# A hybrid decoder layer: 336 series of zero products ahead of the first stage

## The chip, the cores and the metric

The kernel runs on one core of one Trainium2 chip. The metric is the device time of one execution in microseconds. The core has a matrix engine (PE, with its own sequencer that also loads weights, shown as PEld), a vector engine (DVE), a scalar engine (ACT), a general engine (POOL) and a queue engine (SP) that issues transfers. The time of the kernel before is the median of two runs, 1093.47 us (1092.93 to 1094.01).

## The reference

One inference step of one layer, for a prompt group (1 x 512 tokens) and a sample group (8 x 8 tokens) that share weights of width 1024. In float32:

```python
x -> x + post(Wout[concat(Mamba2-SSD heads, mLSTM heads)](pre(x)))   # one combined input projection
  -> x + post(CrossAttn(pre(x), memory K/V))
  -> x + post(SwiGLU(pre(x)))                                        # sandwich RMSNorm everywhere

u = _rms(x) * g_pre_mix
proj = u @ w_in
z, xbc, dt_raw, q, k, v, ig, fg, og = jnp.split(proj, split_at, axis=-1)
xbc, conv_new = causal_conv(xbc, conv_buf, conv_w, conv_b)
```

What matters here is the first step, the normalised input times `w_in`. Both groups are computed together, as 512 + 64 = 576 token columns. Besides the two outputs the step returns the new states and the memory keys and values.

## The kernel before

Activations lie feature-major: 128 partitions by 8 blocks of features by 576 token columns. Each weight matrix is taken in units of 128 x 1024, that is eight 128 x 128 tiles side by side. To reach float32 accuracy with the fast float32r products, a weight `w` is split into `whi` (rounded to float32r, by ACT) and `wlo` (the rest, by DVE or POOL), and the activation `u` likewise into `uh` and `ul`. One block of a matrix product is then three products into one PSUM bank: `whi` with `uh`, `whi` with `ul`, `wlo` with `uh` (lines 202, 203 and 205, in `gemm`; lines 339 to 341 in the first stage). A bank holds 512 float32 columns, so the 576 columns are taken as `HALVES` of 256 and 320, in the feed-forward part as two of 288, and for the values 512 at a time (line 815). No float32r product has a moving operand under 256 columns; the transposes and some small products of the recurrences are plain float32 or bfloat16.

The order at the start is this. DVE writes zeros into a small bfloat16 tile `wz` (line 300), and PE runs 21 products with it into a PSUM tile `ps_warm` that nobody reads (line 303). Meanwhile SP and ACT issue the loads of the parameters, of the input `xraw` by blocks, and of the first two units of `w_in` in quarters (`raws`, lines 304 to 314). ACT and DVE turn each block of the input into `uh` and `ul` (lines 322 and 323) and each quarter of a weight unit into `whi` and `wlo` (line 328, by way of lines 191 and 192). The loop of lines 333 to 341 then runs the first two units' products block by block into four PSUM tiles `ps_in`, and the next unit follows through `gemm`. The rest of the input projection, the convolution, the gates, the recurrences, the output projection, cross attention and the feed-forward part come behind.

SBUF is handed out in numbered slots by the helper `SL`: a tile of a slot waits for the readers of the tile before it in that slot. Slot 1 is first used in the input projection, by `qk` (the queries and keys of the mLSTM heads), when the fifth tile of the convolution is due. PSUM tiles come from rings: `MP` takes one of three banks in turn, `GP` one of three others. The order of instructions on each engine is chosen when the program is built, by a scheduler that simulates a timeline; blocks under `tc.manual_schedule` keep the written order on the engines that they name, and `tc.issue_after` sets an order between two instructions.

```python
    wz = sp.tile([P, 256], BF16, name="wz")
    V.memset(wz, 0.0)
    psw = MP("ps_warm")
    for _ in range(NWARM):
        mm(psw[:, 0:256], wz[:, 0:128], wz, start=True, stop=True, skip_group_check=True)
    S.dma_start(par, I["par"])
```

Of the kernel before, what the change touches and what calls it, by code (L numbers as in the profile page):

```python
# [11 lines left out]
F32 = mybir.dt.float32  # L12
F32R = mybir.dt.float32r
# [6 lines left out]
P = 128  # L20
# [95 lines left out]
def build(nc, tc, ctx, I, O):  # L116
    V, A, G, S, TE = nc.vector, nc.scalar, nc.gpsimd, nc.sync, nc.tensor
    mm = TE.matmul
# [12 lines left out]
    def SL(slot, name, dt=F32, shape=(P, KT, T)):  # L131

        return big.tile(list(shape), dt, name=name, tag="s%d" % slot, bufs=1)
# [5 lines left out]
    def MP(name="m"):  # L139
        return pa.tile([P, 512], F32, name=name, tag="a")  # L140
# [54 lines left out]
    def gemm(ps, units, xh, xl, t0, n, k0=0, k1=None, order=None, late=0):  # L195


        tiles = [(hi[:, j * P:(j + 1) * P], lo[:, j * P:(j + 1) * P]) for hi, lo, nk in units for j in range(nk)]
        order = order or range(len(tiles))
        for i, k in list(enumerate(order))[k0:k1]:  # L200
            (wh, wl), ah, al = tiles[k], xh(k, t0, n), xl(k, t0, n)
            mm(ps, wh, ah, start=i == 0, stop=False)  # L202
            mm(ps, wh, al, start=False, stop=False)  # L203
            for c in range(late) if i == late - 1 else [i] if i >= late else ():
                m = mm(ps, tiles[order[c]][1], xh(order[c], t0, n), start=False, stop=c == len(tiles) - 1)  # L205
        return m
# [94 lines left out]
    psw = MP("ps_warm")  # L301
    for _ in range(NWARM):
        mm(psw[:, 0:256], wz[:, 0:128], wz, start=True, stop=True, skip_group_check=True)
    S.dma_start(par, I["par"])

    wi = [[wp.tile([P, 1024], F32R, name=k, tag=k, bufs=3) for k in ("whi", "wlo")] for _ in range(2)]
    raws = [wp.tile([P, 1024], F32, name="raw", tag="raw", bufs=2) for _ in range(2)]
    for k in range(KT):
        if k % 2 == 0:
            c = slice(128 * k, 128 * k + 256)  # L310
# [42 lines left out]
    stop = gemm(ps0[2][1], [(*w2, KT)], U, UL, 256, 320, 0, NSS)  # L353
# [12 lines left out]
    stop = gemm(ps0[3][0], [(*w3, KT)], U, UL, 0, 256)  # L366
# [343 lines left out]
    for g in range(2):  # L710
        psb = BP("ps_ls")
        pb3 = psb.rearrange("p (h t) -> p h t", h=8)
        for h in range(8):
            mm(psb[:, h * TS:(h + 1) * TS], sel[:80, 8 * g + h:8 * g + h + 1].to_broadcast([80, P]), cumst[:, TP:T],
               start=h == 0, stop=h == 7, skip_group_check=True)
# [8 lines left out]
        for h in range(8):  # L724
            k, j = h % 2, (8 * g + h) // 2
            mm(psi[64 * k:64 * k + 64, j * TS:(j + 1) * TS], xdts[:, 8 * g + h, :], lm[:, h, :], start=True, stop=True,
               skip_group_check=True)
# [12 lines left out]
    for b in range(4):  # L740
# [3 lines left out]
        for g in range(2):  # L744
            for hb in (1, 0):
# [3 lines left out]
                   start=b == 0, stop=b == 3, skip_group_check=True)  # L749
# [139 lines left out]
    for h in range(4):  # L889
# [12 lines left out]
        for c in range(4):  # L902
            mm(pss[:, c * P:(c + 1) * P], k[:, c * P:(c + 1) * P], q[:, c * P:(c + 1) * P], start=True, stop=True,
               skip_group_check=True)
# [39 lines left out]
    for h in range(4):  # L944
        mm(psb[:, h * TS:(h + 1) * TS], sel[:68, h:h + 1].to_broadcast([68, P]), sxst[:, TP:T], start=h == 0, stop=h == 3,
           skip_group_check=True)
# [22 lines left out]
    for hb in range(2):  # L969
# [6 lines left out]
        for b in range(4):  # L976
# [3 lines left out]
            for h in range(4):  # L980
                mm(psn[32 * h:32 * h + 32, 0:257], qpad[:, h, bb, :], c0[:, h, 0:257], start=False, stop=b == 3,
                   skip_group_check=True)
# [1374 lines left out]
```

## Time and profile before

| | before |
|---|---|
| median of 2 runs | 1093.47 us (1092.93 to 1094.01) |
| the profiled execution, as a run | 1092.94 us |
| its span, first to last instruction | 1091.2 us |
| granted clock of PE, mean share | 0.998 |
| products on PE | 8,124 |
| weight loads on PE | 8,124 |
| bytes moved by the DMA queues | 182.29 MB, mean 167 GB/s |

The span is what the trace covers; about 1.7 us of a run lie around it. Busy time counts the stretches in which an engine has an instruction in flight. Products on PE overlap one another, and their ends are modelled, so the busy time of PE tells that there was no hole and not how fast the products followed one another; for that, the distances between their starts are to be read in the timeline. Idle time of an engine that is not the bottleneck costs nothing. In rows of the timeline the first column is the start in microseconds from the start of the span, the second the time from the first start of the row to its last end, and a count (x16) means that neighbouring instructions of one line were merged.

### The profile page before, as it was taken

The page shows a single profiled execution, that of the slowest core. Times are in us where ns is not written, and L with a number is a line of the kernel's source. Part 1 is how long each engine was busy: PE and PEld are TensorE (multiplying, and loading weights), DVE is VectorE, ACT ScalarE, POOL GpSimd, SP SyncE. Part 2 cuts the span into 40 slices and gives each one's busy share as a digit, 9 for nine tenths or more (in the row PEclk, how much of TensorE's full clock was granted, in tenths as well). Part 3 has the DMA queues.
Part 4 walks back from the last instruction along what each step waited for, and adds up shares of the span by engine and source line. Part 5 has one row for each costly group of instructions (what it writes and reads, how often), then busy time and mean ns, then how long its engine had stood idle before and what let it go on. Part 6 is the DMA issues. An engine that isn't in the chain of part 4 may idle for free.

```text
span 1091.2 us, 20715 instructions
## 1 busy us (share of the span) xinstructions
PE 1079.0 (99%) x8124; PEld 1021.6 (94%) x8124; DVE 753.5 (69%) x1507; ACT 611.5 (56%) x1098; POOL 225.2 (21%) x305
## 2 busy tenths in 40 slices
PE   9999999999999999999999999999999999999997
PEld 8999887778999999999988879999999999999997
DVE  6896785758877775569644546666567887787555
ACT  7867632355654555566544545646567566656653
POOL 1332643313213111000244301100011121111000
PEclk9999999999999999999999999999999999999999
DMA  6785634435655348653468765644486687577532
GB/s 206 176 160 127 163 110 172 164 91 172 191 149 154 102 148 287 202 201 114 143 216 278 274 232 175 224 150 100 118 182 146 149 203 170 115 190 183 128 130 88
DMA packets 58966, 182.29 MB, mean 167 GB/s; under 512 B 6604, under 2 KB 11852, under 8 KB 58356
## 3 DMA queue, kind: packets, MB, share of 16 engines
q1 hardware_dynamic: 42740, 138.06, 38.7%
q0 software_dynamic: 15552, 41.95, 19.7%
q8 instruction: 64, 1.05, 0.4%
q10 hardware_dynamic: 576, 0.95, 0.3%
q14 instruction: 34, 0.28, 0.1%
HBM read 160.28 MB, written 20.65 MB: 166 GB/s over the span
## 4 chain that ended last, share of the span: by engine, by line
PE 80%; DVE 6%; DMA 5%; ACT 5%; issue 3%; POOL 1%; SPq 0%; DVEq 0%; ACTq 0%; POOLq 0%
PE ps_in L203 4%; PE ps_in L202 4%; PE ps_in L205 4%; PE ps_v L815 3%; PE ps_g L1849 3%; PE ps_g L1850 3%; PE ps_u L1850 3%; PE ps_u L1851 3%; PE ps_g L1851 3%; PE ps_u L1849 3%; PE ps_dn L1849 2%; PE ps_dn L1850 2%; PE ps_dn L202 2%; PE ps_dn L203 2%; PE ps_dn L1851 2%
## 5 line engine op out<-in xcount | busy, mean ns | idle before, releaser
L202 PE MATMUL ps_in<-uh,whi 128*128 128x320 f32 (+1 forms) x544 | 162.9, 300 | 0.8 <-DVE cb L451 0.5
L205 PE MATMUL ps_in<-uh,wlo 128*128 128x320 f32 (+1 forms) x544 | 162.1, 298 | 0.3 <-DMA wlo<-win 0.3
L203 PE MATMUL ps_in<-ul,whi 128*128 128x320 f32 (+1 forms) x544 | 161.7, 297 | 0.0
L180 ACT CAST whi<-raw 128x1024 fp32r<-128x1024 f32 (+1 forms) x104 | 105.3, 1013 | 97.6 <-PE ps_in L203 25.8
L187 DVE TENSOR_TENSOR wlo<-raw,whi 128x512 fp32r<-128x512 f32 (+1 forms) x96 | 97.2, 1015 | 69.2 <-ACT whi L180 68.3
L202 PEld LDWEIGHTS ps_in<-uh,whi 128*128 128x128 f32 x544 | 102.7, 189 | 3.9 <-issue 1.7
L205 PEld LDWEIGHTS ps_in<-uh,wlo 128*128 128x128 f32 x544 | 102.2, 188 | 1.4 <-DMA wlo<-win 0.5
L203 PEld LDWEIGHTS ps_in<-ul,whi 128*128 128x128 f32 x544 | 102.3, 188 | 0.6
L185 POOL DMA_DIRECT2D wlo<-win x32 | 27.8, 869 | 80.4 <-ACT wlo L184 72.3
L1850 PE MATMUL ps_g<-b,whi 128*128 128x288 f32 x144 | 42.5, 295 | 0.0
L1850 PE MATMUL ps_u<-b,whi 128*128 128x288 f32 x144 | 42.4, 295 | 0.0
L1849 PE MATMUL ps_g<-b,whi 128*128 128x288 f32 x144 | 42.4, 294 | 0.0
L1849 PE MATMUL ps_u<-b,whi 128*128 128x288 f32 x144 | 42.2, 294 | 0.0
L1822 ACT CAST whi<-rawx 128x1024 fp32r<-128x1024 f32 (+1 forms) x26 | 25.6, 985 | 27.2 <-PE ps_dn L1850 13.7
L192 DVE TENSOR_TENSOR wlo<-sw,whi 128x1024 fp32r<-128x1024 f32 (+1 forms) x26 | 29.6, 1140 | 15.7 <-ACT whi L191 15.6
L202 PE MATMUL ps_xo<-qh,whi 128*128 128x288 f32 x128 | 38.7, 304 | 0.2 <-ACT whi L180 0.2
L205 PE MATMUL ps_o<-mixm_h,wlo 128*128 128x256 f32 (+1 forms) x128 | 38.0, 297 | 0.6 <-DVE wlo L187 0.6
L205 PE MATMUL ps_o<-mixs_h,wlo 128*128 128x320 f32 (+1 forms) x128 | 37.7, 295 | 0.0
L203 PE MATMUL ps_xo<-ql,whi 128*128 128x288 f32 x128 | 37.7, 296 | 0.0
L203 PE MATMUL ps_o<-mixs_l,whi 128*128 128x320 f32 (+1 forms) x128 | 37.7, 294 | 0.0
L202 PE MATMUL ps_xq<-u2h,whi 128*128 128x320 f32 (+1 forms) x128 | 37.7, 298 | 0.0
L203 PE MATMUL ps_o<-mixm_l,whi 128*128 128x256 f32 (+1 forms) x128 | 37.7, 294 | 0.0
(765 smaller groups left out, 3836.0 us busy)
## 6 DMA issues: line engine op xcount, KB each, us to landing
raw<-win SPq DMA_DIRECT2D x35, 512.0 KB, 4.0
raw<-wout SPq DMA_DIRECT2D x17, 512.0 KB, 3.6
raw<-wxq SPq DMA_DIRECT2D x13, 512.0 KB, 3.6
raw<-wgate SPq DMA_DIRECT2D x13, 512.0 KB, 3.6
raw<-wup SPq DMA_DIRECT2D x13, 512.0 KB, 5.0
wlo<-win POOLq DMA_DIRECT2D x24, 256.0 KB, 5.0
kva<-kc SPq DMA_DIRECT2D x12, 512.0 KB, 5.7
kva<-vc SPq DMA_DIRECT2D x12, 512.0 KB, 5.7
```

Source lines behind the costliest of these rows:

```text
L180: casts.append(A.copy(hi[:, :n], raw[:, :n]))
L185: G.dma_start(lo[:, a:b], src[:, a:b], accum_op=ALU.add)
L187: e.tensor_tensor(lo[:, a:b], raw[:, a:b], hi[:, a:b].bitcast(F32), op=ALU.subtract)
L192: (eng or V).tensor_tensor(lo, src, hi.bitcast(F32), op=ALU.subtract)
L202: mm(ps, wh, ah, start=i == 0, stop=False)
L203: mm(ps, wh, al, start=False, stop=False)
L205: m = mm(ps, tiles[order[c]][1], xh(order[c], t0, n), start=False, stop=c == len(tiles) - 1)
L815: mm(ps, a, b, skip_group_check=True, **kw)
L1822: A.copy(s.h3[:, s.all], s.r2[:, s.all])
L1849: mm(ps, wh, b[0][k], start=start and k == 0, stop=False, skip_group_check=True)
L1850: mm(ps, wh, b[1][k], start=False, stop=False, skip_group_check=True)
L1851: m = mm(ps, wl, b[0][k], start=False, stop=k == nk - 1, skip_group_check=True)
```

## The change

Behind the 21 products with `wz`, and ahead of the load of the parameters in the program's text, a tile `bench` of 4,608 float32r columns is taken in slot 1 and filled with zeros by DVE. A list of 336 series is made up. Each series is 21 products of a 128 x 128 stationary tile and a moving operand of `n` columns, both out of `bench`, into one more PSUM tile, `ps_probe`. Nobody reads that tile.

A series is `(mode, n, moving offsets, weight offsets)`. With mode 1 the moving columns are read from the last to the first, and the bank is written from the last column to the first as well. Within a series the moving start steps by 576 columns and the weight start by 128 after every three products, as the blocks of the input projection do; the offsets are added to these starts, taken in turn. There are three families. The first has both modes, widths of 256, 288, 320 and 512, and eight moving offsets from 0 to 56 in steps of 8 (64 series). The second has mode 0, eight further widths from 128 to 448, and two offsets (16). The third has both modes at 288 and 320 columns, with a pattern of three products: the second product reads at another moving offset than the first and third, and the third takes another weight offset, all 64 combinations of four offsets each (256). In all there are 7,056 products. They stand under `tc.manual_schedule` for PE.

```diff
+    bench = SL(1, "bench", F32R, (P, 4608))
+    V.memset(bench.bitcast(F32), 0.0)
+    SEG = []
+    for mode in range(2):
+        for n in (256, 288, 320, 512):
+            for d in range(0, 64, 8):
+                SEG.append((mode, n, (d,), (0,)))
+    for n in (128, 192, 224, 240, 272, 304, 384, 448):
+        for d in (0, 16):
+            SEG.append((0, n, (d,), (0,)))
+    for mode, n in ((0, 288), (0, 320), (1, 288), (1, 320)):
+        for a in (0, 16, 32, 48):
+            for b in (0, 16, 32, 48):
+                for c in (0, 16, 32, 48):
+                    SEG.append((mode, n, (a, b, a), (0, 0, c)))
+
+    def span(a, n, back):
+        t_ = bench[:, a:a + n]
+        return t_[:, ::-1] if back else t_
+
+    pq = MP("ps_probe")
+    with tc.manual_schedule(engines={TE.engine}):
+        for mode, n, ms_, ws_ in SEG:
+            for i in range(21):
+                a = 64 + ms_[i % len(ms_)] + 576 * (i // 3 % 4)
+                b = 2944 + ws_[i % len(ws_)] + 128 * (i // 3 % 8)
+                mm(pq[:, 0:n][:, ::-1] if mode & 1 else pq[:, 0:n], bench[:, b:b + P], span(a, n, mode & 1),
+                   start=i < 2, stop=True, skip_group_check=True)
     S.dma_start(par, I["par"])
```

## The prediction

> **What bounds the kernel now.** I read the page's busy table first, then the clock row, then PE's waits, then the start by stages, and last the distance between products of one shape.
>
> ```profile
> span 1091.2 us, 20715 instructions
> PE 1079.0 (99%) x8124; PEld 1021.6 (94%) x8124; DVE 753.5 (69%) x1507; ACT 611.5 (56%) x1098; POOL 225.2 (21%) x305
> PEclk9999999999999999999999999999999999999999
> ...
> PE ps_warm L303 <- DVE wz L300: 1.1, 1, 1.1
> PE ps_o L205 <- DVE wlo L187: 0.6, 1, 0.6
> PE ps_in L202 <- DVE cb L451: 0.5, 1, 0.5
> ...
> PE ps_v L797 <- POOL wlo L187: 0.2, 1, 0.2
> ```
>
> PE is busy for 1079.0 of 1091.2 us at the full granted clock; the other engines have at least 31% of the span free. The third view is PE's waits, longest in total first (total, times, longest): after the one at the start none is over 0.6 us. So PE has 12.2 us in which it does nothing, and a product added to it is paid in full unless it falls into one of those holes. That decides the sign: what is added here is only PE work, and a lot of it.
>
> The start, by stages (length, then busy time and count of each engine, the clock, the DMA share and GB/s):
>
> ```profile
> 0.00:5.42 5.42, 3.97 (x21) 2.75 (x22) 1.25 (x5) 3.00 (x7) 1.01 (x10) 1.00 0.66 206
> 5.42:18.01 12.59, 12.59 (x95) 12.59 (x96) 10.02 (x19) 9.86 (x18) 0.97 (x3) 1.00 1.00 348
> 18.01:40.00 21.99, 21.34 (x164) 20.27 (x163) 16.91 (x34) 14.86 (x24) 6.57 (x22) 1.00 0.44 117
> ```
>
> PE's first product of real work starts at 5.42 us, when the first weights have been cast, and from there PE is never idle up to 18.01 though the DMA queues are full (share 1.00). From 18.01 to 40 it idles 0.65 us. Delaying this stage therefore lets all its loads and casts finish early, and that is worth no more than this 0.65 us.
>
> **How long a product takes.** The duration column is of no use here (products overlap; a 128x288 one is drawn 0.29 us long while the next starts 0.13 us later). I take the distance between starts in the timeline of PE, first and last row of unbroken runs:
>
> ```profile
> 493.61 0.28 PE L202 MATMUL ps_mk<-memhl,wmh 128*128 128x256 f32 x1
> ...
> 499.14 0.28 PE L205 MATMUL ps_mk<-memhl,wml 128*128 128x256 f32 x1
> ...
> 799.75 0.30 PE L1851 MATMUL ps_g<-b,wlo 128*128 128x288 f32 x1
> ...
> 802.95 0.29 PE L1851 MATMUL ps_u<-u3h,wacc 128*128 128x288 f32 x1
> ...
> 398.93 0.30 PE L202 MATMUL ps_o<-mixs_h,whi 128*128 128x320 f32 x1
> ...
> 402.25 0.31 PE L205 MATMUL ps_o<-mixs_h,wlo 128*128 128x320 f32 x1
> ...
> 72.69 0.31 PE L202 MATMUL ps_in<-uh,whi 128*128 128x320 f32 x1
> ...
> 76.07 0.31 PE L205 MATMUL ps_in<-uh,wlo 128*128 128x320 f32 x1
> ...
> 207.59 0.40 PE L815 MATMUL ps_v<-whi,uh 128*128 128x512 f32 x1
> ...
> 208.97 0.39 PE L815 MATMUL ps_v<-whi,ul 128*128 128x512 f32 x1
> ...
> 100.21 1.06 PE L599 MATMUL ps_cb<-bc 128*128 128x128 f32 x8
> ```
>
> - 256 columns: 48 products, (499.14 - 493.61) / 47 = 0.1177 us.
> - 288: 25 products, (802.95 - 799.75) / 24 = 0.1333; I take 0.133.
> - 320: two runs of 24, 3.32 / 23 = 0.1443 and 3.38 / 23 = 0.1470. The same shape differs by 2% with the tiles it reads; I take the middle, 0.1455.
> - 512: seven products, 1.38 / 6 = 0.230.
> - 128 columns under a full 128-column weight: eight in 1.06 us, the last drawn 0.27 long, 0.79 / 7 = 0.113, no faster than 256 columns. Each product loads its own weights (as many weight loads as products in the busy table), so below 256 columns the weight load sets the pace. I take 0.112.
>
> All are float32r runs but the last, and all read the moving operand forwards.
>
> **The change part by part.** Removed: nothing. Moved: in the changed kernel's own order three products of the first stage (256, 320 and 256 columns) stand ahead of the 7,056 new ones, the rest of that stage behind; further on a handful of casts and loads change places with neighbours on DVE, ACT, POOL and SP, none past a stage, at nothing.
>
> Added, the products. 336 series of 21 make 7,056. By width: 16 series of 256, 144 of 288, 144 of 320, 16 of 512, and two each of 128, 192, 224, 240, 272, 304, 384 and 448; that is 336, 3,024, 3,024 and 336 products, and 42 of each other width. Half the 256, 288, 320 and 512 ones run backwards (3,360). Nothing reads the bank they write, and no engine but PE works for them, so no product waits for another engine. Their sum:
>
> - 256: 336 x 0.1177 = 39.5 us
> - 288: 3,024 x 0.133 = 402.2
> - 320: 3,024 x 0.1455 = 440.0
> - 512: 336 x 0.230 = 77.3
> - 128 to 240: 168 x 0.112 = 18.8
> - 272, 304, 384, 448, between the rows of their neighbours (0.125, 0.139, 0.174, 0.202): 42 x 0.640 = 26.9
>
> Together 1,004.7 us for 2,188,704 columns, 0.459 ns a column. The offsets of 8, 24 and 40 columns are not seen in the trace, and the 2% between the two runs of 320 shows that addresses count. I bound the pace by the quickest and the slowest run I find:
>
> ```profile
> 139.11 1.09 PE L644 MATMUL ps_yi<-lm,xdt 128*64 128x128 f32 x16
> ...
> 1042.73 0.31 PE L202 MATMUL ps_dn<-hh,wdh 128*128 128x320 f32 x1
> ...
> 1060.94 0.31 PE L205 MATMUL ps_dn<-hh,wdl 128*128 128x320 f32 x1
> ...
> L616 PE MATMUL ps_h<-xe,btok x16: 590/592/697, 110.4 to 210.1; 128*128 128x512 f32 x16
> ...
> L815 PE MATMUL ps_v<-whi,uh x80: 388/392/586, 167.2 to 239.2; 128*128 128x512 f32 x80
> ```
>
> The first, 16 products of 128 columns under half a weight, takes (1.09 - 0.27) / 15 = 0.0547 us each, 0.427 ns a column; at that pace the new products take 2,155,776 x 0.427 ns + 18.8 = 939 us (the narrow ones stay with their weight load). The second, 120 products of 320 with some short stalls, takes 18.21 / 119 = 0.153, 0.478 ns a column: 1,046 us. I stay with 1,005, because it comes from the runs of the same shapes.
>
> The Trainium skill has a rule against this sum ("TensorE: Matmul & The Clock Gate", Back-to-back issue gap): warm products follow each other every N/2.4 + 2.5 ns. By that an estimate for the series is 2,188,704 / 2.4 + 7,056 x 2.5 ns = 930 us, and the time 2,022. The trace disagrees for this data type: at 288 columns that rule gives 122.5 ns, and the row above shows 133.
>
> Added, the zeros. One DVE memset of 4,608 float32 columns behind that of `wz`. The trace has none that long. From below it costs nothing that PE sees; from above, DVE's longest simple row
>
> ```profile
> L187 DVE TENSOR_TENSOR wlo<-raw,whi 128x1024 fp32r<-128x1024 f32 x1 | 1.2, 1225 | 1.6 <-ACT whi L180 1.6
> ```
>
> gives 4.5 x 1.225 = 5.5 us from about 1.0, so the series start at the latest at 6.5 us, where three ahead of them would have let them start at 5.42 + 3 x 0.13 = 5.8. That is 0 to 0.7 us on the path. DVE's first steps behind the memset (the `ul` of the first rows) come up to 2 us later, but the products that read them now wait behind a thousand us of series. Against it stands the 0.65 us of idle time that the delay fills. I book the two as zero.
>
> Added, space: `bench` lies where `qk` is written later, long after PE has read the last zero, and `ps_probe` takes one of three turns of a PSUM ring whose other turns were free. No wait comes from either.
>
> The profiled execution took 1092.94 us as a run (span 1091.2 and 1.7 around it), 0.5 below the median 1093.47 of the two runs. So 1092.9 + 1004.7 + 0 = 2,097.6; I say 2,097.
>
> **The rivals.**
>
> *Backwards is slow.* Every row of the trace reads and writes with step +1. If a step of -1 halves the rate of reading the moving columns or of writing the bank, it is paid by 3,360 products, whose forward price is 168 x (0.1177 + 0.133 + 0.1455 + 0.230) + 1,344 x 0.2785 = 479 us. The nearest slow rows are plain float32's above: each of its two passes (16 records for 8 products) is drawn 592 - 392 = 200 ns longer than a float32r product of the same width, 0.430 against 0.230, a factor of 1.87. Then +417 us, 2,514 us; at both passes, 3.74, +1,312 and 3,410. For it: no row excludes it. Against it: neighbours in memory stay neighbours. It would be a step at the boundary between forward and backward series, and decides as soon as the factor is over 1.1. The Trainium skill ("PSUM — Partial Sum Buffer", Specifications (TRN2)) says that a non-contiguous pattern slows matmuls significantly; whether a descending one counts it does not say, and no run here shows it.
>
> *Narrow float32r products leave the fast mode.* No float32r row is under 256 columns. If those 168 run like plain float32 (2 x 0.430 / 512 = 1.68 ns a column), their 32,928 columns take 55.3 us in place of 18.8: 2,134 us.
>
> *The quicker pace of the page*, 2,022 us. It needs the distances in the rows to come from other engines' traffic, which is gone during most of the series. Against it: the 144.3 ns of one set of tiles and 147.0 of another repeat whatever else runs.
>
> *Nothing runs, not slower.* No instruction reads `ps_probe`. If what stands between program and chip drops products without a reader, only the 0.7 us of the memset stays: 1,093 us. It decides if products of the kind are missing from PE's count of instructions. Against it: `ps_warm`, which nobody reads either, has its 21 products in the stage 0.00:5.42.
>
> **How the numbers follow.** Forecast, all widths and both directions near the rows' pace: 0.70, 2,097 us, between 1092.9 + 939 = 2,032 and 1092.9 + 1,046 = 2,139. Narrow products slow: 0.14, at 2,134, up to 2,139 + 37 = 2,176. Backwards slow: 0.11. Page's pace: 0.04. Nothing runs: 0.01. The first two hold 0.84, so the range is theirs, 2,032 to 2,176. A measurement of this kernel can tell about 2% from no change; all cases but the last are slower by far more: slower 0.99, same 0.01, faster 0.
>
> **What would show it.** In the page of the changed kernel: about 7,000 more products on PE, with busy time of some 2,080 us; a timeline in which 288-column series step by 0.13 us and 320-column ones by 0.145, the same in the first 672 products as in the 672 backward ones behind them; in the stage windows, DVE, ACT and the DMA queues silent from about 30 us to the end of the series; the first real stage behind them, and everything after it as long as before. A step between the two directions proves the forecast wrong on its largest term; 42 products of 240 columns that take longer than 42 of 272 show the narrow mode; series that start after 6.5 us show that the memset was mis-sized.

## The result and the profile after

The changed kernel takes 2098.86 us (median of two runs, 2098.50 to 2099.22) against 1093.47 before: a ratio of 1.9194, with a 95% interval from 1.9112 to 1.9277. The profiled execution took 2099.22 us as a run. The forecast was 2,097.

The page after, with DVE's row of slices beside the rows that were shown of before:

```profile
span 2097.4 us, 34832 instructions
PE 2086.9 (99%) x15180; PEld 2014.1 (96%) x15180; DVE 757.3 (36%) x1508; ACT 611.1 (29%) x1098; POOL 225.2 (11%) x305
DVE  3000000000000000000287668775765476587866
PEclk9999999999999999999999999999999999999999
```

PE's longest waits after, in total, number and longest of them, in us:

```profile
PE ps_warm L303 <- DVE wz L300: 1.1, 1, 1.1
PE ps_in L205 <- DMA wlo<-win: 0.6, 1, 0.6
PE ps_in L202 <- DVE cb L480: 0.6, 1, 0.6
```

PE has 7,056 products more (15,180 - 8,124) and is busy for 1,007.9 us more; DVE, ACT and POOL have the same busy time as before within 4 us (DVE's 3.8 are the memset). DVE's row of slices has one 3, then 18 zeros, then work to the end. The clock stays full, and PE's waits are as short as they were.

The series in PE's timeline after, with the rows on either side (start and length in us, then the shape of the first of them):

```profile
5.69 1.06 PE L368 MATMUL ps_in<-uh,whi 128*128 128x256 f32 x3
6.55 1007.49 PE L331 MATMUL ps_probe<-bench 128*128 128x256 f32 x7056
1013.87 0.28 PE L369 MATMUL ps_in<-ul,whi 128*128 128x256 f32 x1
```

The view by windows after, for the stretch in which nothing but the series runs (the window, its length, then busy time and number for PE, weight load, DVE, ACT and POOL, the granted clock, the DMA share and its GB/s):

```profile
30.00:1013.87 983.87, 983.87 (x6863) 968.14 (x6862) 0.00 (x0) 0.00 (x0) 0.00 (x0) 1.00 0.00 1
```

From the first product of the series to the first one behind them are 1013.87 - 6.55 = 1007.32 us, without a hole. The span grew by 2097.4 - 1091.2 = 1006.2, so everything else together became 1.1 us shorter: the series start about 0.7 us later than the 5.8 us at which the forecast had them without the memset, and the rest runs 1.8 us faster than before.

By width, grouped by line and shape (busy time of the whole group in us, mean duration of one in ns):

```profile
L331 PE MATMUL ps_probe<-bench 128*128 128x320 f32 x3024 | 444.0, 309 | 0.0
L331 PE MATMUL ps_probe<-bench 128*128 128x288 f32 x3024 | 401.0, 295 | 0.0
L331 PE MATMUL ps_probe<-bench 128*128 128x512 f32 x336 | 78.6, 396 | 0.0
L331 PE MATMUL ps_probe<-bench 128*128 128x256 f32 x336 | 40.1, 281 | 0.0
L331 PE MATMUL ps_probe<-bench 128*128 128x240 f32 x42 | 4.9, 274 | 0.0
L331 PE MATMUL ps_probe<-bench 128*128 128x128 f32 x42 | 4.8, 274 | 0.0
```

Here busy time is usable for once, because the groups stand in unbroken blocks: each block counts only the tail of its last product too much, about 0.16 us (at 288 columns there are four blocks). A 288-column product therefore costs 401.0 / 3,024 = 0.1326 us, while its drawn duration is 0.295.

### The profile page after: what moved, and what is told of

It reads as the page before. It is cut to its first block, busy times and chain, and to the rows that moved or that the text cites. A ratio compares the mean times of both kernels' runs of the same rounds, so it can differ in the third digit from the quotient of the medians.

```text
span 2097.4 us, 34832 instructions
## 1 busy us (share of the span) xinstructions
PE 2086.9 (99%) x15180; PEld 2014.1 (96%) x15180; DVE 757.3 (36%) x1508; ACT 611.1 (29%) x1098; POOL 225.2 (11%) x305
## 4 chain that ended last, share of the span: by engine, by line
PE 96%; ACT 1%; DVE 1%; issue 1%; DMA 1%; POOL 0%; DVEq 0%; ACTq 0%; POOLq 0%; SPq 0%
PE ps_probe L331 48%; PE ps_in L203 3%; PE ps_in L202 3%; PE ps_in L205 3%; PE ps_v L844 2%; PE ps_o L205 2%; PE ps_o L203 2%; PE ps_g L1878 2%; PE ps_g L1879 2%; PE ps_o L202 2%; PE ps_u L1879 2%; PE ps_u L1880 2%; PE ps_g L1880 2%; PE ps_u L1878 2%; PE ps_dn L1878 1%; PE ps_dn L1879 1%
## 5 line engine op out<-in xcount | busy, mean ns | idle before, releaser
L331 PE MATMUL ps_probe<-bench 128*128 128x288 f32 (+6 forms) x7056 | 1007.5, 306 | 0.0
L331 PEld LDWEIGHTS ps_probe<-bench 128*128 128x128 f32 x7056 | 991.7, 188 | 15.7
```

Source lines behind the costliest of these rows:

```text
L331: mm(pq[:, 0:n][:, ::-1] if mode & 1 else pq[:, 0:n], bench[:, b:b + P], span(a, n, mode & 1), start=i < 2, stop=True, skip_group_check=True)
```

## The experiments

Where no interval is given, the kernel ran once. The runs with bfloat16, with 64 weight columns, with real numbers and with two banks shared one run of the kernel before, 1094.62 us.

### The same products on two-byte operands

```diff
-    bench = SL(1, "bench", F32R, (P, 4608))
-    V.memset(bench.bitcast(F32), 0.0)
+    bench = SL(1, "bench", BF16, (P, 4608))
+    V.memset(bench, 0.0)
```

> The 7,056 products read bfloat16 zeros in place of float32r ones; counts, widths, order and places stay. In the changed kernel the series took 1,007 us, about 13 ns a product more than one column each 1/2.4 ns. If that surplus belongs to the 4-byte operands, a 288-column product falls from 132.5 to about 122.5 ns, a 512-column one from 233 to 216, the series to about 930 us and the run from 2,099 to about 2,022. If every product with weights of its own pays it, whatever the type, the series stay at 1,007 us and the run at 2,099.

Measured: 2021.02 us. The series in PE's timeline of this run:

```profile
6.12 929.77 PE L331 MATMUL ps_probe<-bench 128*128 128x256 bf16 x7056
935.62 0.39 PE L369 MATMUL ps_in<-ul,whi 128*128 128x256 f32 x1
```

The groups of 288 and 128 columns in the same run:

```profile
L331 PE MATMUL ps_probe<-bench 128*128 128x288 bf16 x3024 | 371.1, 286 | 0.0
L331 PE MATMUL ps_probe<-bench 128*128 128x128 bf16 x42 | 2.5, 219 | 0.0
```

The series take 935.62 - 6.12 = 929.5 us. Read off the distances of all starts, a 288-column product takes 122.5 ns and a 512-column one 215.8. The Trainium skill ("TensorE: Matmul & The Clock Gate", Back-to-back issue gap) has N/2.4 + 2.5 ns for the gap of what it calls an isolated product, which gives 122.5 and 215.8: for bfloat16 the trace agrees to the digit, though every product here loads weights of its own. The same stream in float32r takes 132.4 and 233. So the page's rule, which the forecast set aside for the rows of the trace, is right here for one data type and 8% short at 288 columns for the other.

### Fewer weight columns: 64, and 16

```diff
-                mm(pq[:, 0:n][:, ::-1] if mode & 1 else pq[:, 0:n], bench[:, b:b + P], span(a, n, mode & 1),
+                mm(pq[0:64, 0:n][:, ::-1] if mode & 1 else pq[0:64, 0:n], bench[:, b:b + 64], span(a, n, mode & 1),
```

> Every product of the series has 64 weight columns in place of 128 (64 output rows); widths, counts and order stay. If the weight load sets the pace below 256 columns, as the forecast had it, the 128-column products fall from 111 to 55-60 ns, those of 192 to 80-95. If the surplus of 13 ns at 288 columns and more comes from the load too, those fall as well, to about 122-128 ns at 288, the series to 925-965 us and the run to 2,017-2,057. If the surplus belongs to the moving operand or to the change from one product to the next, 288 columns stay at 132 ns, only the narrow widths save 3 to 5 us, and the run is about 2,094. If narrow float32r products had left the fast mode without our seeing it, the narrow ones would not move at all.

Measured with 64 columns: 2092.33 us. With 16 in place of 64 on the same line:

> As the series with half weights, but with 16 weight columns in each product. With 64 columns the forward 288-column product took 131.4 ns (132.3 with 128), the 512-column one 229.8 (232.5). If the surplus over n/2.4 ns is the moving operand's own, 288 stays at 130-132 ns and the series at 990-1,000 us. If reading weights at the same time causes it, an eighth of the weight columns brings 288 to 122-125 ns and the series to 925-945 us.

Measured with 16: 2090.23 us, beside 1092.58 of the kernel before (median of 14 runs). The groups of 288 and 128 columns, with 64 weight columns:

```profile
L331 PE MATMUL ps_probe<-bench 128*64 128x288 f32 x3024 | 399.0, 294 | 0.0
L331 PE MATMUL ps_probe<-bench 128*64 128x128 f32 x42 | 2.7, 223 | 0.0
```

The same groups with 16 weight columns:

```profile
L331 PE MATMUL ps_probe<-bench 128*16 128x288 f32 x3024 | 397.9, 294 | 0.0
L331 PE MATMUL ps_probe<-bench 128*16 128x128 f32 x42 | 2.7, 222 | 0.0
```

Two things part here. The 128-column products fall from 4.8 us for 42 to 2.7: by their starts from 111 to 60 ns, and no further with 16 columns. So a full float32r weight load is the floor below 256 moving columns, as the forecast had it. The 288-column products hardly move, from 401.0 to 399.0 and 397.9 us, though the weight load has shrunk to an eighth. The series as a whole, from its first start to the start behind it, falls from 1007.3 us to 999.5 with 64 columns and 997.9 with 16. So the float32r surplus over bfloat16 is not the price of reading weights at the same time, which can account for 1 of some 10 ns a product at 288 columns. It goes with the moving side or with the data type in the array; these runs do not part those two.

### Real numbers, in another place

```diff
-    bench = SL(1, "bench", F32R, (P, 4608))
-    V.memset(bench.bitcast(F32), 0.0)
+    bench = ul.rearrange("p k t -> p (k t)")
```

The whole block is moved behind the loop over the input's loads.

> The series read the low half ul of the input (8 x 576 columns of real numbers) in place of zeros; the memset goes, and the block stands behind the loads of the input, so that it starts when the last block of ul is there, at about 15 us, with some products of the first stage ahead of it. If the price of a product does not depend on what it multiplies, the series take 1,007 us again at the full granted clock and the run is 2,096 to 2,104. If zeros were the cheap case (less power, a clock granted without limit), the series take longer: at a clock of 0.81 they would take 1,240 us and the run 2,330.

Measured: 2099.41 us, mean clock 0.999. The main row of the series in PE's timeline, and the product behind them:

```profile
16.22 1005.94 PE L355 MATMUL ps_probe<-ul 128*128 128x256 f32 x7044
1022.00 0.31 PE L369 MATMUL ps_in<-uh,wlo 128*128 128x320 f32 x1
```

The 288-column group of this run:

```profile
L355 PE MATMUL ps_probe<-ul 128*128 128x288 f32 x3024 | 401.0, 295 | 0.0
```

Twelve products of the series stand a little earlier, so this row has 7,044. The 288-column group takes the same 401.0 us as with zeros. Zeros and these real numbers cost the same, and the place makes no difference either: with part of the first stage ahead of them the run is 0.6 us longer. That is within the spread of single runs: the kernel before moved between 1091.46 and 1095.36 us over 17 runs.

### Two banks in turn

```diff
-    pq = MP("ps_probe")
+    pqs = [MP("ps_probe"), GP("ps_probe")]
...
+                pq = pqs[i % 2]
...
-                   start=i < 2, stop=True, skip_group_check=True)
+                   start=i < 4, stop=True, skip_group_check=True)
```

> Neighbouring products of a series write two PSUM banks in turn instead of one. If the 13 ns surplus came from adding into the bank that the product before is still writing, 288 columns fall from 132.5 to about 122.5 ns, the series to about 930 us, the run to 2,022. If the bank does not matter, the series stay within 3 us of 1,007 and the run within 5 us of 2,099.

Measured: 2099.69 us, and the series again take 1013.17 - 5.86 = 1007.31 us:

```profile
5.86 1007.47 PE L332 MATMUL ps_probe<-bench 128*128 128x256 f32 x7056 [0.36 <-DVE ghalf L426]
1013.17 0.28 PE L369 MATMUL ps_in<-uh,whi 128*128 128x256 f32 x1
```

Adding into the bank that the product before has just written costs nothing. In this build no real product stands ahead of the series, and they start 0.36 us after PE ran out of work. The row names `ghalf`, a short DVE step right behind the memset, which is over at 5.81 us here too: this is the memset on the path.

### The zeros alone, by DVE and by POOL

The change without its products; only this is left:

```diff
+    bench = SL(1, "bench", F32R, (P, 4608))
+    V.memset(bench.bitcast(F32), 0.0)
```

> Only the tile of zeros and its memset are left of the change, without any product. If the products are the whole price, what stays is the late start of the first stage: the first product of real work at 5.7 us in place of 5.4, the products that need ul behind it later by up to 1.1 us, part of it given back by the idle time before 40 us; 1,093.5 to 1,094.8 us, a ratio of 1.000 to 1.001. If the memset or the space it takes disturbs the stages behind (another order, a wait for the slot), the loss is some microseconds: 1,096 or more.

Measured in five rounds: 1090.88 us against 1092.66, a ratio of 0.9986 (0.9975 to 0.9996). Neither expectation held: it is faster by 1.8 us, though the first stage starts later in its trace. DVE's timeline of this run:

```profile
1.91 3.90 DVE L306 MEMSET bench<- 128x4608 f32 x1 [0.91 <-issue]
```

And PE's, the first products of real work:

```profile
6.10 0.83 PE L342 MATMUL ps_in<-uh,whi 128*128 128x256 f32 x4 [0.84 <-ACT whi L191]
```

The first real product comes at 6.10 us in place of 5.42, so some 2.5 us were won further on. That the start is the memset's doing is not shown: the product waited for a cast on ACT, and ACT for the load of `par`, until 4.59 us in place of 3.77. The order of the instructions shows where the gain could come from: with the memset on DVE the scheduler, which simulates a timeline, arrives at another order of the convolution and the gates on all engines; PE, for one, runs the transposes into `ps_ct` 13 products later than before. With the memset on POOL (`G.memset` in place of `V.memset`) no engine's order differs from before, so this tells the order from the tile:

> The tile of zeros again without any product, but POOL writes it, which has nothing to do at that time. Every other instruction then stands in the order of the kernel before on every engine. With zeros by DVE the time was 0.9986 of before (0.9975 to 0.9996), against the 1.000 to 1.001 expected. If that 0.14% came from the other order that the scheduler chose around DVE's memset, it is gone here: 0.9995 to 1.0005. If it came from the tile itself, the ratio is 0.9986 again.

Measured in five rounds: 1093.12 us against 1092.58, a ratio of 1.0006 (0.9996 to 1.0015), which leaves out 0.9986. The tile and its slot win nothing. What is left for the 1.8 us is the other order, possibly together with DVE's delay that brought it about; the order was not tried without the memset. The traces fit the order. On DVE and ACT it differs between 30.7 and 94.8 us, and lined up product by product the run is 0.99 us behind the kernel before at 30 us and 1.36 ahead at 150. Three stalls of PE that the trace before has at 37.3, 95.4 and 109.8 us (0.62, 0.81 and 0.60 us from one start to the next), and the run with POOL nearly alike (0.61, 0.95 and 0.61), are steps of 0.12 to 0.15 us here.

## Why the prediction was right

**The bound.** PE was read as the engine that pays for every product in full, and it did: 1007.32 us of series, 1006.2 us of span. No other engine took part, as the windows show.

**The price by distance of starts.** The terms of the sum against the series, summed over the distances of all starts of the trace after:

| columns | products | forecast, us | measured, us |
|---|---|---|---|
| 256 | 336 | 39.5 | 39.8 |
| 288 | 3,024 | 402.2 | 400.4 |
| 320 | 3,024 | 440.0 | 443.3 |
| 512 | 336 | 77.3 | 78.3 |
| 128 to 240 | 168 | 18.8 | 18.8 |
| 272 to 448 | 168 | 26.9 | 26.8 |
| sum | 7,056 | 1,004.7 | 1,007.3 |

The largest error is at 320, where the middle of two runs (0.1443 and 0.1470) was taken; the series stand at 0.1466, near the upper one. That the time came out within 2 us is partly luck: the series were booked 2.6 us too short, and what else changed, booked at nothing, gave 1.1 back. Had the drawn durations been used, 288 columns alone would have come to 3,024 x 0.295 = 892 us, more than twice too much.

**Addresses.** The offsets that the trace before did not show were bounded by the quickest and slowest runs, 939 to 1,046 us. They matter little for the sum: by their starts, the 16 plain series at 288 columns lie between 131.1 and 133.5 ns a product, the 128 patterned ones between 131.0 and 133.6; at 320 columns the plain ones lie between 146.6 and 147.3, the patterned ones between 144.5 and 148.8. That spread of 3% is not noise: in the run with real numbers, out of another tile, series by series the pace differs from this one by at most 0.05 ns behind the first series, which was interrupted. With bfloat16 there is no such spread at 288 columns (122.5 in all 144). The lower of the two bounds, though, was misread. The 16 records of `ps_yi` are the two passes each of eight plain float32 products, and by their starts they come in pairs, 6 ns apart, every 109 ns; half of 109 is not the pace of a product.

**Backwards.** The rival with 0.11 fell. The first family by shape, in the window of its forward half:

```profile
L331 PE MATMUL ps_probe<-bench 128*128 128x512 f32 x168 | 39.2, 394 | 0.0
L331 PE MATMUL ps_probe<-bench 128*128 128x320 f32 x168 | 24.8, 309 | 0.0
L331 PE MATMUL ps_probe<-bench 128*128 128x288 f32 x168 | 22.5, 295 | 0.0
L331 PE MATMUL ps_probe<-bench 128*128 128x256 f32 x168 | 20.1, 281 | 0.0
```

The same family in the window of its backward half:

```profile
L331 PE MATMUL ps_probe<-bench 128*128 128x512 f32 x169 | 39.8, 397 | 0.0
L331 PE MATMUL ps_probe<-bench 128*128 128x320 f32 x168 | 24.8, 310 | 0.0
L331 PE MATMUL ps_probe<-bench 128*128 128x288 f32 x168 | 22.3, 295 | 0.0
L331 PE MATMUL ps_probe<-bench 128*128 128x256 f32 x168 | 20.0, 282 | 0.0
```

The backward window caught one 512-column product of the forward half more; apart from that the rows agree within 1%. Over all four widths, in the first and third families together, the forward half takes 480.4 us and the backward half 481.4. A step of -1, in the read and in the write together, costs here what a step of +1 does.

**Narrow products.** The rival with 0.14 fell too: 42 products of 128 columns took 4.8 us, where plain float32 would have cost 42 x 128 x 1.68 ns = 9.0; and 240 columns cost what 128 do. The runs with 64 and 16 weight columns show that it is the weight load which holds them at 111 ns. The row from which the forecast took its 0.112 could not show that. The eight records of `ps_cb` are two passes each of four plain float32 products; a pass of 512 columns took 0.430 us in the trace before, 0.84 ns a column, and at that pace one of 128 columns takes 0.108 with no weight load in the way. That the term of 18.8 us came out to the digit was therefore luck, and its mechanism was shown only afterwards.

**The page's pace.** It fell for the reason given, though not quite in the form given. The rival's condition was that traffic of other engines makes the distances long; in the stretch 30.00:1013.87 there is none, and the distances stay. The bfloat16 run shows that the page's rule is right for that type.

**Nothing runs.** The 7,056 products stand in PE's row.

**The small terms.** The start and the cover were booked as 0 together, from 0 to 0.7 us late and 0.65 us given back. The start took the full 0.7. The cause was not the one that was forecast: the memset was over at 5.81 us, and the first product of the series came at 6.55, right behind the three real ones. So the sign that the forecast gave for a mis-sized memset, a start after 6.5, appeared without its cause. The three had come late and slowly. Their first started at 5.69 instead of 5.42, since its weights' cast on ACT began 0.27 us later, and from one start to the next they and the first two of the series took 0.378, 0.266, 0.214, 0.213 and 0.150 us, where before the first took 0.223 and the next ones 0.12 to 0.15. PE was slow already in the products that nobody reads. After:

```profile
1.06 4.66 PE L303 MATMUL ps_warm<-wz 128*128 128x256 bf16 x21 [1.06 <-DVE wz L300]
```

Before:

```profile
1.06 3.97 PE L303 MATMUL ps_warm<-wz 128*128 128x256 bf16 x21 [1.06 <-DVE wz L300]
```

The same 21 products take 4.66 us in place of 3.97, because PE has two paces. By the distances of their starts, these 256-column products follow each other every 213 ns at first and every 109 ns later, and every trace changes over once in its first 7 us: the kernel before at about 4.1 us, the changed one at about 6.8, during the second product of the series. The slow pace holds for float32r too (0.214 for 256 columns, 0.266 for 320). In the run with bfloat16 series, where PE had changed over before them, the three real products took 6.12 - 5.59 = 0.53 us in place of 0.86. So of the 0.7 us some 0.3 are the late cast, another 0.3 the slow pace, and the rest the first product, which the forecast had at 0.13. The moment of the change-over does not come from the added products: over the nine traces it lies anywhere between 4.0 and 6.8 us, and the runs with 64 and 16 weight columns, which are built alike up to the series, have it at 6.7 and 4.7. What sets it was not tried; the granted clock of the view by windows is 1.00 from the start and does not show it.

The give-back was under-sized: behind the series the first stages run without the stalls they had, as the view by windows after shows.

```profile
1013.87:1026.50 12.63, 12.63 (x98) 12.63 (x97) 0.00 (x0) 1.35 (x3) 0.00 (x0) 1.00 0.01 1
1026.50:1048.00 21.50, 21.50 (x168) 21.00 (x167) 13.64 (x32) 12.21 (x19) 6.76 (x16) 1.00 0.53 138
```

About the same work that took 18.01:40.00 with 0.65 us of idle time before is now without a hole, and lined up product by product it gains 1.2 us up to 48 us of the old time: PE's idle column does not count a stall in which the last product is still drawn. The remaining 0.5 us of the 1.8 are the balance of single stalls of 0.3 to 0.8 us between 75 and 610 us of the old time, of both signs; the largest, 0.8 at 459 us, stands in the trace before alone and in neither run of the zeros without products, and they were not followed up. It is not the other order of the run with the zeros alone: in the changed kernel DVE, ACT and POOL keep the order of before from 31 us of the old time on.

## What to carry to other kernels

Where one engine has no holes, work added to it is priced by count times distance between starts, taken from unbroken runs of the same shape and type in the same trace; drawn durations were over twice that at 288 columns (0.295 against 0.132 us). A rule that is exact for one data type was 8% off for another here, so the nearest row comes first; and a row must be of the same type, for one of plain float32 counts passes and not products. When an experiment changes less than 0.2%, compare the built order of instructions first: a scheduler may answer to one added memset with another order on all engines, and that can weigh more than the memset.

## What the runs showed that was not expected

- For bfloat16 the distance of products with weights of their own is n/2.4 + 2.5 ns at every width from 128 to 512 (55.8 ns at 128, 215.8 at 512), so a full bfloat16 weight load is no floor there. For float32r it is 132.4 at 288 and 146.6 at 320, about n/2.4 + 13 (the surplus is 11.8 at 256 and 19.6 at 512), and a full weight load holds it at 110 to 112 below 256.
- A memset of 128x4608 float32 takes 3.90 us on DVE and 3.94 on POOL, 0.85 ns a column; the forecast's upper bound from a two-input row was 5.5.
- The pace of float32r products depends by up to 3% on the offsets of their operands (144.5 to 148.8 ns at 320 columns), and each series repeats its own pace from run to run.
- For its first 4.0 to 6.8 us, by the trace, PE runs at about half its later pace (213 against 109 ns for 256 bfloat16 columns), while the granted clock reads 1.00.
- A memset on DVE, with no product added, made the kernel 0.14% faster (0.9975 to 0.9996), most likely by way of the order that the scheduler chose after it.
